# A tile's three partial products as three 256-column matmuls into one PSUM region, in place of 512 + 256 columns and a later add

## The chip, the core and the metric

The kernel runs on one NeuronCore of one Trainium2 chip. The metric is the device time of one execution in microseconds (us); three runs of the kernel before lie between 1150.1 and 1150.66 us, with a median of 1150.5 us. The profiler recorded one execution of its own, instruction by instruction.

## What is computed

One transformer-like layer on 256 rows of 2048 features, in float32 (B = 1, S = 256). Nearly all the arithmetic is in four weight matrices: `w_in` (2048 x 6676), `w_out` (2048 x 2048), `w_up` (2048 x 8192), `w_down` (8192 x 2048).

```python
h = rmsnorm(x, norm_mix)
proj = h @ w_in + b_in
...
x = x + jnp.concatenate([y_m, y_a, y_c], axis=-1) @ w_out
h2 = rmsnorm(x, norm_ffn)
x = x + jnp.square(jax.nn.relu(h2 @ w_up)) @ w_down
return rmsnorm(x, final_norm)
```

`y_m`, `y_a` and `y_c` are a chunked mLSTM of 8 heads, a forgetting attention of 4 heads and a convolution branch, all made from slices of `proj`.

## The kernel before

**Split operands.** A product has to come out to nearly float32 accuracy, while TensorE is fed the type fp32r. So every operand is split in a high part `hi` and a low part `lo` (the rest), and a product a·w is made of three partial products: a_hi·w_hi, a_lo·w_hi and a_hi·w_lo. The weights come from DRAM in pieces of 1 MiB (`unit`), by DMAs from the queue of SyncE. ScalarE copies half a piece to `hi` (line 368), VectorE subtracts to get `lo` (line 387). The activations are kept in a tile `big[name]` of 16 chunks (128 features each) by 512 columns: 256 rows' high parts, then the same 256 rows' low parts.

**Two kinds of block.** `Block` is a run of output columns that is accumulated in PSUM over the whole contraction; `matmuls` (lines 397 to 422) emits half a piece of it. In a block of kind A the activations are stationary and 512 columns of weights move; three matmuls of 512 columns go into one PSUM bank, two of them with the same stationary operand. In a block of kind B the weights are stationary (128 x 128 at a time, index `f`) and the activations move; the result is transposed, features by rows. Kind B serves the convolution branch, the queries and keys, the mLSTM's operands (all from `w_in`, blocks 256 wide, operand `x`) and the whole of `w_up` (blocks 512 wide, operand `h`). For each `f` and each chunk `k` a block of kind B issues two matmuls:

```python
mul(ps, hi[:, ii, f * P:(f + 1) * P], stat[:, k, :], s0, False)
mul(ps[:, 0:S], lo[:, ii, f * P:(f + 1) * P], stat[:, k, 0:S], False, s1)
```

The first streams all 512 columns (high and low rows) past w_hi, the second 256 columns past w_lo. Columns 0 to 255 of the bank then hold two of the partial products, columns 256 to 511 the third. So each `f` takes a bank of its own, and `join` (lines 434 to 453) adds the halves: ScalarE copies columns 256 to 511 to a tile `tmp` with bias and scale (line 441 or 443), VectorE adds columns 0 to 255 (line 447). For `w_up` four such joins make the tile `z`, VectorE makes relu(z)·z (line 1131), and the result is split again into the tile `hid`.

**Order of the work.** The kernel's own list scheduler (`task`, `best`, `issue`, `force`) gives each task to an engine at a time that it estimates from costs written in the code. The stream of weight pieces sets TensorE's order; small TensorE tasks (transposes, attention scores) are put between half pieces when their operands are expected to be there. PSUM has eight banks, in two rotations of four, `mm` and `mx`. Up to five split half pieces are held (`NHL`), and four raw pieces (`NRAW`).

Of the kernel before, what the change touches and what calls it, by code (L numbers as in the profile page):

```python
# [9 lines left out]
AF = mybir.ActivationFunctionType  # L10
# [23 lines left out]
def trunk(ctx: ExitStack, tc, x, norm_mix, w_in, b_in, mlstm_conv_w, mlstm_conv_b,  # L34
# [23 lines left out]

    # ---- emission: a list schedule on estimated engine clocks
    clock = dict(act=0.0, dve=0.0, pool=0.0, pe=0.0, ctl=0.0)  # L60
# [5 lines left out]
    class Buf:  # L66
        """One tile of a rotation of n: taken when the tile n before it has no readers left."""
        def __init__(self, rot):
# [39 lines left out]
    def room(takes):  # L108
        """When the buffers are free; None while a reader of the old tile is not yet issued."""
        r = 0.0  # L110
        for b in takes:
            h = b.rot.hist
            if len(h) >= b.rot.n:
                for u in h[len(h) - b.rot.n].readers:
                    if u.fin is None:
                        return None
                    r = max(r, u.fin + LAT)
        return r
# [54 lines left out]
    def extras():  # L173
        """TensorE tasks whose operands are there by now."""
        while True:
            run(clock["pe"])
            p = best("pe")
            if not p or p[2] > clock["pe"] - MARGIN:
                return
            issue(p[1], p[2])  # L180
# [12 lines left out]

    # ---- pools
    pools = {}
# [19 lines left out]

    # ---- loads of x, parameter rows
    RAWN = 8 * 272
# [31 lines left out]

    # x lies where the values and the attention operands come later  # L250
    xt = [sbt(pl("mix"), [P, 2 * NH * (HD + 1)], "x0", tag="vaug")[:, 0:D], sbt(pl("mix"), [P, D], "x1", tag="fqk")]
# [4 lines left out]

    # ---- constants
    ident = sbt(base, [P, P], "ident")
# [29 lines left out]
    def small(n=2):  # L288
        """Columns of the tile of statistics."""
        nst[0] += n  # L290
        return st[:, nst[0] - n:nst[0]]
# [3 lines left out]

    # ---- weight stream
    units = []

    class Block:
        def __init__(self, kind, w, st, key, tag="mm"):  # L300
            self.kind, self.w, self.st, self.key, self.tag = kind, w, st, key, tag
            self.n = 2 if kind == "A" else w // P
            self.bufs = [Buf(mm_rot if tag == "mm" else mx_rot) for _ in range(self.n)]
            self.done = [Task("pe", 0.0, None) for _ in range(self.n)]
            self.started = False
            self.need = {}

    def unit(b, src, c0, k0, last, gates=0, gside=None):
        """One MiB of weights: columns c0.. of src (and the gate columns beside them)."""
        n = 4 if b.w == 512 else 8  # L310
        units.append(dict(b=b, src=src, c0=c0, ks=list(range(k0, k0 + n)), w=b.w,
                          g=gates, gside=gside, last=last, first=not b.started))
        b.started = True
# [43 lines left out]
    def split_tasks(i, deps):  # L357
        """High and low parts of half a unit."""
        u, h = divmod(i, 2)
# [37 lines left out]
    def matmuls(i, toks):  # L397
        u, half = divmod(i, 2)
        d = units[u]
        b = d["b"]  # L400
        w = d["w"]
        n = len(d["ks"])
        stat = b.st()
        hi, lo = hl[i]
        for ii in range(n // 2):
            kk = half * (n // 2) + ii
            k = d["ks"][kk] % KC
            s0 = d["first"] and kk == 0
            s1 = d["last"] and kk == n - 1
            if b.kind == "A":  # L410
                for j in toks:
                    xh = stat[:, k, j * P:(j + 1) * P]
                    xl = stat[:, k, S + j * P:S + (j + 1) * P]
                    ps = b.bufs[j].t
                    mul(ps, xh, hi[:, ii, :], s0, False)
                    mul(ps, xh, lo[:, ii, :], False, False)
                    mul(ps, xl, hi[:, ii, :], False, s1)
            else:
                for f in range(w // P):
                    ps = b.bufs[f].t  # L420
                    mul(ps, hi[:, ii, f * P:(f + 1) * P], stat[:, k, :], s0, False)
                    mul(ps[:, 0:S], lo[:, ii, f * P:(f + 1) * P], stat[:, k, 0:S], False, s1)

# [6 lines left out]
    big_tile("y")  # L430
    chunk = {}   # tasks that make chunk k of a stationary or moving operand

    # rows of the transposed products, halves summed: out = s * (ps_a + ps_b) + bias
    def join(o, b, i, bias=None, s=1.0, prio=0, deps=(), takes=()):
        t = Buf(tmp_rot)
        pb = b.bufs[i]

        def f1():
            t.t = sbt(base, [P, S], "tmp", bufs=3)
            if bias is None:  # L440
                act.activation(t.t, pb.t[:, S:2 * S], AF.Copy)
            else:
                act.activation(t.t, pb.t[:, S:2 * S], AF.Identity, bias=bias, scale=s)  # L443

        def f2():
            if s == 1.0:
                dve.tensor_add(o(), t.t, pb.t[:, 0:S])
            else:
                dve.scalar_tensor_tensor(o(), pb.t[:, 0:S], s, t.t, op0=OP.mult, op1=OP.add)

        a = t_act(ca(S, True), f1, [b.done[i], col_tasks if bias is not None else None], prio=prio - 2,
                  takes=[t], uses=[pb])
        return t_dve(cd(S), f2, [a] + list(deps), prio=prio - 2, takes=takes, uses=[pb, t])

    # ---- parameter columns
    def cols_task(name, r0, r1, deps, prio=-3):
# [9 lines left out]

    # the array's clock rises once it is kept busy: transposes of the identity while x arrives
    def warm_up():
# [7 lines left out]

    # ---- x: norm, transpose, split
    xs_stat = [small(4) for _ in range(2)]
# [59 lines left out]

    # ---- late constants and parameters
    vb = {}  # L540
# [55 lines left out]

    # ---- values
    def blk(*a, **kw):
# [25 lines left out]

    # ---- conformer branch
    u_rot, g_rot = Rot(1), Rot(1)
# [99 lines left out]

    # ---- the other values, forgetting attention's operands
    b = block_units(blk("A", 512, xs, "x"), w_in, C_V + 512)
# [15 lines left out]

    # ---- gates
    gps, gsum, gtp = mx_buf(), mx_buf(), mx_buf()
# [13 lines left out]
    def build_gates():  # L760
# [11 lines left out]
        a_l = t_act(c1, lambda: act.activation(gl, gu, AF.Ln), [d_u], prio=3, table="ln")  # L772
        # log1p(e) = ln(u) + (e - (u - 1)) / u with u = fl(1 + e)
        d = t_dve(0.45, lambda: dve.scalar_tensor_tensor(ge, gu, -1.0, ge, op0=OP.add, op1=OP.subtract), [d_u], prio=3)
# [38 lines left out]

    # ---- heads, both kinds
    pw_rot, pt_rot, hh_rot = Rot(2), Rot(2), Rot(2)

    def head_out(num, nb, r, r_task, num_task, prio, put):
        """Root mean square norm of r * num by rows, transposed; put() takes the columns."""
        sq, t, sc = small(), small(), small()
# [30 lines left out]

    # ---- forgetting attention
    def fox(h, prio):
# [4 lines left out]
        def scores():  # L857
            q, k = hold["fqk"][:, h // 2, h % 2, :], hold["fqk"][:, 2 + h // 2, h % 2, :]
            ps = sb.t = bank("mx")
            # F[l] is constant along a row and leaves its softmax as it is: -F[s] and the mask are added  # L860
            mul(ps[:, 0:384], sel[:, NH + h:NH + h + 1].to_broadcast([P, P]), em, True, False)
            mul(ps[:, P:384], identb, mask_f.rearrange("p a b -> p (a b)"), False, False)
            mul(ps[:, 0:S], q[:, P:S], k, False, False)
            mul(ps[:, S:384], q[:, 0:P], k[:, 0:P], False, True)
# [39 lines left out]

    # ---- mLSTM
    xpad = [None, None]
# [124 lines left out]

    # ---- after the mixer
    ob = [blk("A", 512, ys, "y") for _ in range(4)]
# [66 lines left out]

    # ---- feed-forward layer, by quarters of the hidden features
    z_rot, zz_rot = Rot(2), Rot(2)
# [11 lines left out]
    for q in range(4):  # L1114
        down_of = []
        for c in range(4):
            b = block_units(blk("B", 512, lambda: big["h"], "h", tag()), w_up, 2048 * q + 512 * c)
            zb, wb = Buf(z_rot), Buf(zz_rot)

            def o_z(i, zb=zb):  # L1120
                if i == 0:
                    zb.t = sbt(pl("late"), [P, 4, S], "z", bufs=2)
                return zb.t[:, i, :]

            js = [late_open]
            for i in range(4):
                js.append(join(lambda i=i, o_z=o_z: o_z(i), b, i, takes=[zb] if i == 0 else [], deps=[js[-1]]))

            def f1(zb=zb, wb=wb):
                wb.t = sbt(pl("late"), [P, 4, S], "zz", bufs=2)  # L1130
                dve.scalar_tensor_tensor(wb.t, zb.t, 0.0, zb.t, op0=OP.max, op1=OP.mult)

# [62 lines left out]

    # ---- issue
    NU = len(units)
# [79 lines left out]
```

## Time and profile before

| | |
|---|---|
| Median of three runs | 1150.5 us |
| Span of the profiled execution, first to last instruction | 1148.2 us |
| TensorE (PE) busy | 1133.9 us, 99% |
| Weight loads (PEld) busy | 965.3 us, 84% |
| VectorE (DVE) busy | 717.3 us, 62% |
| ScalarE (ACT) busy | 574.3 us, 50% |
| Mean granted TensorE clock | 0.996 of full speed |
| Share of PE in the chain that ended last | 97% |

The profile gives the profiled execution by its span; the median of the runs is 2.3 us longer, which is taken here as what lies around the span. Every matmul shows as two records: a load of the stationary operand (LDWEIGHTS, under PEld) and the matmul (MATMUL, under PE). Records of matmuls overlap, since they are pipelined, so the length of a record is not what it costs: the cost in a stream is the distance from one start to the next.

### The profile page before, as it was taken

What the parts mean: (1) busy time and instruction counts of PE and PEld (TensorE: products, weight loads), DVE (VectorE), ACT (ScalarE), POOL (GpSimd) and SP (SyncE); (2) the same over time, 40 slices, a digit from 0 to 9 for tenths busy, and PEclk for the clock granted to TensorE, in tenths of its full rate; (3) what the DMA queues carried; (4) which work ended last, traced back from release to release, by engine and by line L of the source; (5) the groups of instructions that cost most, each with busy time, mean ns of one, the idle gap of its engine ahead of it and who ended that gap; (6) DMA issues with size and microseconds to landing.
All of it is one profiled execution on the core that took longest, in us unless ns stands there. A gap on an engine that the chain in (4) does not pass through costs nothing.

```text
span 1148.2 us, 14812 instructions
## 1 busy us (share of the span) xinstructions
PE 1133.9 (99%) x5880; PEld 965.3 (84%) x5880; DVE 717.3 (62%) x978; ACT 574.3 (50%) x807; POOL 17.6 (2%) x40
## 2 busy tenths in 40 slices
PE   8999999999999999999999999999999999999996
PEld 7888888888888888888888888888888888888885
DVE  6679988886665556556545655544655554566553
ACT  6455366777864545444344444333544333454442
POOL 1000000000000000000000000000000000000000
PEclk9999999999999999999999999999999999999999
DMA  8756654557546556655566655566655566655542
GB/s 304 242 184 191 199 164 148 151 153 248 169 162 220 184 185 184 190 199 196 184 189 193 189 193 190 184 191 195 189 193 187 184 192 199 190 189 184 183 147 74
DMA packets 127692, 214.91 MB, mean 187 GB/s; under 512 B 3676, under 2 KB 44936, under 8 KB 127240
## 3 DMA queue, kind: packets, MB, share of 16 engines
q1 hardware_dynamic: 127016, 212.92, 57.9%
q8 instruction: 46, 0.75, 0.3%
q10 hardware_dynamic: 608, 1.06, 0.3%
q14 instruction: 22, 0.18, 0.0%
HBM read 211.87 MB, written 2.10 MB: 186 GB/s over the span
## 4 chain that ended last, share of the span: by engine, by line
PE 97%; DMA 1%; issue 0%; ACT 0%; DVE 0%; SPq 0%; POOL 0%; POOLq 0%; ACTq 0%; DVEq 0%
PE mm L57 64%; PE mx L57 32%; DMA x<-in_x_dram 1%; PE mx L1085 0%; SPq L255 0%; PE mx L846 0%; POOL st L294 0%; PE mx L531 0%; ACT x2t L1188 0%; PE mx L879 0%; DVE lo L387 0%; ACT junk L1175 0%; POOLq L1272 0%; ACT hi L368 0%; PE mx L705 0%
## 5 line engine op out<-in xcount | busy, mean ns | idle before, releaser
L387 DVE TENSOR_TENSOR lo<-raw,hi 128x1024 fp32r<-128x1024 f32 x392 | 480.1, 1225 | 384.8 <-ACT hi L368 383.4
L368 ACT ACTIVATE hi<-raw 128x1024 fp32r<-128x1024 f32 x392 | 415.5, 1061 | 507.4 <-PE mm L57 317.8
L57 PE MATMUL mm<-x,hi 128*128 128x512 f32 x640 | 227.8, 400 | 0.0
L57 PE MATMUL mm<-h,hi 128*128 128x512 f32 x512 | 180.7, 397 | 0.0
L57 PE MATMUL mx<-h,hi 128*128 128x512 f32 x512 | 180.4, 397 | 0.0
L57 PE MATMUL mm<-x,lo 128*128 128x256 f32 x640 | 179.4, 280 | 0.0
L57 PE MATMUL mm<-hi,hid 128*128 128x512 f32 x512 | 159.0, 389 | 0.0
L57 PE MATMUL mx<-hi,hid 128*128 128x512 f32 x512 | 158.9, 389 | 0.0
L57 PEld LDWEIGHTS mm<-x,hi 128*128 128x128 f32 x640 | 120.2, 188 | 28.9 <-ACT tmp L443 0.4
L57 PE MATMUL mm<-h,lo 128*128 128x256 f32 x512 | 143.7, 281 | 0.0
L57 PE MATMUL mx<-h,lo 128*128 128x256 f32 x512 | 143.7, 281 | 0.0
L57 PEld LDWEIGHTS mm<-x,lo 128*128 128x128 f32 x640 | 120.9, 189 | 0.1
L57 PEld LDWEIGHTS mm<-h,hi 128*128 128x128 f32 x512 | 96.1, 188 | 23.3 <-DVE x2t L1073 0.2
L57 PEld LDWEIGHTS mx<-h,hi 128*128 128x128 f32 x512 | 96.1, 188 | 23.3
L57 PEld LDWEIGHTS mm<-hi,hid 128*128 128x128 f32 x512 | 96.1, 188 | 20.1
L57 PEld LDWEIGHTS mx<-hi,hid 128*128 128x128 f32 x512 | 96.1, 188 | 20.0
L57 PE MATMUL mm<-lo,hid 128*128 128x512 f32 x256 | 99.6, 389 | 0.0
L57 PE MATMUL mx<-lo,hid 128*128 128x512 f32 x256 | 99.6, 389 | 0.0
L57 PEld LDWEIGHTS mm<-h,lo 128*128 128x128 f32 x512 | 96.7, 189 | 0.2
L57 PEld LDWEIGHTS mx<-h,lo 128*128 128x128 f32 x512 | 96.7, 189 | 0.0
L57 PE MATMUL mm<-hi,y 128*128 128x512 f32 x256 | 80.4, 392 | 0.0
L57 PE MATMUL mm<-hi,x 128*128 128x512 f32 x192 | 61.6, 396 | 0.0
(191 smaller groups left out, 872.6 us busy)
## 6 DMA issues: line engine op xcount, KB each, us to landing
raw<-in_w_up_dram SPq DMA_DIRECT2D x64, 1024.0 KB, 5.3
raw<-in_w_down_dram SPq DMA_DIRECT2D x64, 1024.0 KB, 5.2
raw<-in_w_in_dram SPq DMA_DIRECT2D x45, 1024.0 KB, 5.3
raw<-in_w_out_dram SPq DMA_DIRECT2D x16, 1024.0 KB, 5.3
raw<-in_w_in_dram SPq DMA_DIRECT2D x4, 1032.0 KB, 5.1
raw<-in_w_in_dram SPq DMA_DIRECT2D x2, 1088.0 KB
x<-in_x_dram SPq DMA_DIRECT2D x8, 256.0 KB, 6.0
x2t<-in_x_dram SPq DMA_DIRECT2D x2, 1024.0 KB
```

Of the source, the lines that this page charges most:

```text
L57: pe.matmul(o, l, r, start=start, stop=stop, skip_group_check=True)
L368: act.activation(t, raws[u][0][:, h * n:(h + 1) * n, :], AF.Copy)
L387: dve.tensor_sub(hl[i][1], raws[u][0][:, h * n:(h + 1) * n, :], hl[i][0].bitcast(F32))
```

## The change

Blocks of kind B issue three matmuls of 256 columns per `f` and `k`, all into the same 256 columns of PSUM: w_hi past the high rows, w_hi past the low rows, w_lo past the high rows. Two `f` share a bank, so a block takes half as many banks. `join` becomes one ScalarE activation with bias and scale, straight from PSUM to its target. For `w_up` ScalarE applies Relu to two `f` at once (512 columns), and VectorE squares with a plain product.

```diff
         def __init__(self, kind, w, st, key, tag="mm"):
             self.n = 2 if kind == "A" else w // P
-            self.bufs = [Buf(mm_rot if tag == "mm" else mx_rot) for _ in range(self.n)]
+            banks = 2 if kind == "A" else self.n // 2
+            self.bufs = [Buf(mm_rot if tag == "mm" else mx_rot) for _ in range(banks)]
...
                 for f in range(w // P):
-                    ps = b.bufs[f].t
-                    mul(ps, hi[:, ii, f * P:(f + 1) * P], stat[:, k, :], s0, False)
-                    mul(ps[:, 0:S], lo[:, ii, f * P:(f + 1) * P], stat[:, k, 0:S], False, s1)
+                    ps = b.bufs[f // 2].t[:, (f % 2) * S:(f % 2 + 1) * S]
+                    wh, wl = (t[:, ii, f * P:(f + 1) * P] for t in (hi, lo))
+                    mul(ps, wh, stat[:, k, 0:S], s0 and f % 2 == 0, False)
+                    mul(ps, wh, stat[:, k, S:2 * S], False, False)
+                    mul(ps, wl, stat[:, k, 0:S], False, s1)
...
-    def join(o, b, i, bias=None, s=1.0, prio=0, deps=(), takes=()):
-        t = Buf(tmp_rot)
-        pb = b.bufs[i]
+    def join(o, b, i, bias, s=1.0, prio=0, deps=(), takes=()):
+        pb = b.bufs[i // 2]
         def f1():
-            t.t = sbt(base, [P, S], "tmp", bufs=3)
-            if bias is None:
-                act.activation(t.t, pb.t[:, S:2 * S], AF.Copy)
-            else:
-                act.activation(t.t, pb.t[:, S:2 * S], AF.Identity, bias=bias, scale=s)
-
-        def f2():
-            if s == 1.0:
-                dve.tensor_add(o(), t.t, pb.t[:, 0:S])
-            else:
-                dve.scalar_tensor_tensor(o(), pb.t[:, 0:S], s, t.t, op0=OP.mult, op1=OP.add)
+            act.activation(o(), pb.t[:, (i % 2) * S:(i % 2 + 1) * S], AF.Identity, bias=bias, scale=s)
...
-            for i in range(4):
-                js.append(join(lambda i=i, o_z=o_z: o_z(i), b, i, takes=[zb] if i == 0 else [], deps=[js[-1]]))
+            for i in range(2):
+                def f0(i=i, zb=zb, pb=b.bufs[i]):
+                    if i == 0:
+                        zb.t = sbt(pl("late"), [P, 4, S], "z", bufs=2)
+                    act.activation(zb.t[:, 2 * i:2 * i + 2, :], pb.t.rearrange("p (c s) -> p c s", c=2), AF.Relu)
...
-                dve.scalar_tensor_tensor(wb.t, zb.t, 0.0, zb.t, op0=OP.max, op1=OP.mult)
+                dve.tensor_mul(wb.t, zb.t, zb.t)
```

TensorE, at the start of the first `w_up` block (`mm` is a PSUM bank, `h` the activations, `hi` and `lo` the weights' parts, then partitions x columns of the output); before:

```order
L57 MATMUL mm<-hi,y 128x512
L57 MATMUL mm<-h,hi 128x512
L57 MATMUL mm<-h,lo 128x256
L57 MATMUL mm<-h,hi 128x512
L57 MATMUL mm<-h,lo 128x256
```

and with the change:

```order
L57 MATMUL mm<-hi,y 128x512
L57 MATMUL mm<-h,hi 128x256 x2
L57 MATMUL mm<-h,lo 128x256
L57 MATMUL mm<-h,hi 128x256 x2
L57 MATMUL mm<-h,lo 128x256
```

Each matmul of 512 columns has become two of 256; the built program has 7475 matmul instructions where it had 5811, that is 1664 more. Around the blocks the small tasks of the mixer stand a few half pieces earlier or later, and their number is the same.

VectorE, at the end of the first `w_up` block (`z` holds a block's sums, `zz` the squares, `hid` the split result); before:

```order
L387 TENSOR_TENSOR lo<-raw,hi 128x1024 x6
L447 TENSOR_TENSOR z<-tmp,mm 128x256 x4
L1131 SCALAR_TENSOR_TENSOR zz<-z 128x1024
L387 TENSOR_TENSOR lo<-raw,hi 128x1024 x2
L1137 TENSOR_TENSOR hid<-zz,hid 128x4x256
```

and with the change (line 388 is the former 387, 1124 the former 1131, 1130 the former 1137):

```order
L388 TENSOR_TENSOR lo<-raw,hi 128x1024 x6
L1124 TENSOR_TENSOR zz<-z 128x1024
L388 TENSOR_TENSOR lo<-raw,hi 128x1024 x2
L1130 TENSOR_TENSOR hid<-zz,hid 128x4x256
```

The four additions are gone and the square stays in its place.

ScalarE at the same place; before:

```order
L368 ACTIVATE hi<-raw 128x1024 x6
L441 ACTIVATE tmp<-mm 128x256 x4
L368 ACTIVATE hi<-raw 128x1024 x2
L1135 ACTIVATE hid<-zz 128x4x256
```

and with the change:

```order
L369 ACTIVATE hi<-raw 128x1024 x6
L1117 ACTIVATE z<-mm 128x512 x2
L369 ACTIVATE hi<-raw 128x1024 x2
L1128 ACTIVATE hid<-zz 128x4x256
```

Four copies of 256 columns have become two activations of 512, between the same splits.

## Rows read from the trace of the kernel before

**Rows 1.** The page's first part: busy us (share of the span) and instructions.
```profile
PE 1133.9 (99%) x5880; PEld 965.3 (84%) x5880; DVE 717.3 (62%) x978; ACT 574.3 (50%) x807; POOL 17.6 (2%) x40
```

**Rows 2.** Waits of PE, then of PEld: us in total, times, longest.
```profile
PE mx L531 <- DVE x L511: 3.6, 1, 3.6
...
PEld mm L57 <- DVE lo L387: 0.6, 1, 0.6
```

**Rows 3.** The page's costliest groups: xcount | busy us, mean ns of a record.
```profile
L57 PE MATMUL mm<-x,hi 128*128 128x512 f32 x640 | 227.8, 400 | 0.0
...
L57 PE MATMUL mx<-h,hi 128*128 128x512 f32 x512 | 180.4, 397 | 0.0
...
L57 PE MATMUL mm<-hi,hid 128*128 128x512 f32 x512 | 159.0, 389 | 0.0
...
L57 PEld LDWEIGHTS mm<-hi,hid 128*128 128x128 f32 x512 | 96.1, 188 | 20.1
```

**Rows 4.** The chain that ended last: start us, us, what, xmatmuls.
```profile
207.99 16.96 PE mm L57 x96
...
272.98 8.32 PE mm L57 x48
...
346.24 1.34 PE mx L57 x12
...
452.89 22.19 PE mx L57 x128
...
541.25 21.76 PE mx L57 x96
...
629.13 22.61 PE mx L57 x128
```

**Rows 5.** Timeline of PE from 500 us: start us, length us, what.
```profile
500.10 0.28 PE L57 MATMUL mx<-h,lo 128*128 128x256 f32 x1
500.22 0.39 PE L57 MATMUL mx<-h,hi 128*128 128x512 f32 x1
500.45 0.28 PE L57 MATMUL mx<-h,lo 128*128 128x256 f32 x1
500.57 0.39 PE L57 MATMUL mx<-h,hi 128*128 128x512 f32 x1
```

**Rows 6.** Timeline of PE from 650.4 us.
```profile
650.40 0.28 PE L57 MATMUL mx<-h,lo 128*128 128x256 f32 x1
650.52 0.40 PE L57 MATMUL mx<-h,hi 128*128 128x512 f32 x1
650.76 0.28 PE L57 MATMUL mx<-h,lo 128*128 128x256 f32 x1
650.88 0.40 PE L57 MATMUL mx<-h,hi 128*128 128x512 f32 x1
```

**Rows 7.** Timeline of the weight loads (PEld) from 500 us.
```profile
500.11 0.19 PEld L57 LDWEIGHTS mx<-h,hi 128*128 128x128 f32 x1
500.22 0.19 PEld L57 LDWEIGHTS mx<-h,lo 128*128 128x128 f32 x1
```

**Rows 8.** Groups by form, ScalarE and VectorE at the joins.
```profile
L1131 DVE SCALAR_TENSOR_TENSOR zz<-z 128x1024 f32<-128x1024 f32 x16 | 19.6, 1225 | 0.5
...
L443 ACT ACTIVATE tmp<-mm,colp 128x256 f32<-128x256 f32 x36 | 15.3, 472 | 17.7 <-PE mm L57 17.7
...
L447 DVE TENSOR_TENSOR z<-tmp,mm 128x256 f32<-128x256 f32 x32 | 11.8, 422 | 0.0
L441 ACT ACTIVATE tmp<-mx 128x256 f32<-128x256 f32 x32 | 11.5, 385 | 6.5 <-PE mx L57 6.5
...
L937 ACT ACTIVATE mqk<-mqk 128x512 f32<-128x512 f32 x8 | 5.0, 624 | 0.0
```

**Rows 9.** Timeline of PE from 346 us.
```profile
346.08 1.50 PE L57 MATMUL mx<-vaug,pt 128*128 128x129 f32 x12
347.33 0.48 PE L57 MATMUL mm<-hi,y 128*128 128x512 f32 x1
```

More of the change, by code (lines that the diff above doesn't have):

```diff
@@ L431, in trunk @@
     chunk = {}
-    def join(o, b, i, bias=None, s=1.0, prio=0, deps=(), takes=()):
-        t = Buf(tmp_rot)
-        pb = b.bufs[i]
+    def join(o, b, i, bias, s=1.0, prio=0, deps=(), takes=()):
+        pb = b.bufs[i // 2]
         def f1():
-            t.t = sbt(base, [P, S], "tmp", bufs=3)
-            if bias is None:
-                act.activation(t.t, pb.t[:, S:2 * S], AF.Copy)
-            else:
-                act.activation(t.t, pb.t[:, S:2 * S], AF.Identity, bias=bias, scale=s)
-        def f2():
-            if s == 1.0:
-                dve.tensor_add(o(), t.t, pb.t[:, 0:S])
-            else:
-                dve.scalar_tensor_tensor(o(), pb.t[:, 0:S], s, t.t, op0=OP.mult, op1=OP.add)
-        a = t_act(ca(S, True), f1, [b.done[i], col_tasks if bias is not None else None], prio=prio - 2,
-                  takes=[t], uses=[pb])
-        return t_dve(cd(S), f2, [a] + list(deps), prio=prio - 2, takes=takes, uses=[pb, t])
+            act.activation(o(), pb.t[:, (i % 2) * S:(i % 2 + 1) * S], AF.Identity, bias=bias, scale=s)
+        return t_act(ca(S, True) + 0.09, f1, [b.done[i], col_tasks] + list(deps), prio=prio - 2, takes=takes,
+                     uses=[pb])
     def cols_task(name, r0, r1, deps, prio=-3):
@@ L1118, in trunk @@
             zb, wb = Buf(z_rot), Buf(zz_rot)
[L1120 to L1123, printed above, removed]
             js = [late_open]
-            for i in range(4):
-                js.append(join(lambda i=i, o_z=o_z: o_z(i), b, i, takes=[zb] if i == 0 else [], deps=[js[-1]]))
+            for i in range(2):
[3 more added lines that the diff above has]
+                    act.activation(zb.t[:, 2 * i:2 * i + 2, :], pb.t.rearrange("p (c s) -> p c s", c=2), AF.Relu)
+                js.append(t_act(ca(512, True), f0, [b.done[2 * i], b.done[2 * i + 1], js[-1]], prio=-2,
+                                takes=[zb] if i == 0 else [], uses=[b.bufs[i]]))
             def f1(zb=zb, wb=wb):
                 wb.t = sbt(pl("late"), [P, 4, S], "zz", bufs=2)
-                dve.scalar_tensor_tensor(wb.t, zb.t, 0.0, zb.t, op0=OP.max, op1=OP.mult)
+                dve.tensor_mul(wb.t, zb.t, zb.t)
             d = t_dve(cd(1024), f1, js[1:], prio=-1.9, takes=[wb], uses=[zb])
```

## Prediction, made before the changed kernel ran

> **What bounds the kernel.** I read the page's busy shares first: PE is busy 99% of the span, VectorE 62%, ScalarE 50% [rows 1]. Records of matmuls overlap, so a busy PE alone proves little; the waits settle it. In the whole execution PE waited once for longer than 2 us, for the first scaled rows of x at the start, and no weight load of the main stream waited longer than 0.6 us for a split weight [rows 2]. So nothing feeds TensorE too late, and the end is set by how many matmuls it has to stream and how far apart they start. The chain that ended last gives that distance, since its pieces are unbroken runs of one kind [rows 4].
>
> Kind A, 512 columns each: 96 matmuls in 21.76 us, so 226.7 ns apart [rows 4]. Kind B runs in two rhythms. In the first quarter of `w_up` 64 pairs of 512 + 256 columns take 22.19 us, 346.7 ns a pair; in the later quarters 22.61 us, 353.3 ns a pair [rows 4]. The blocks of `w_in` show the same two (8.32 us for 24 pairs is 346.7 ns, 16.96 us for 48 pairs is 353.3 ns) [rows 4]. There are 640 + 512 + 512 = 1664 pairs, with as many of `mm<-h,hi` as of `mx<-h,hi` [rows 3]. Going through the chain I count 400 at 346.7 ns (256 in the first quarter, 144 in `w_in`) and 1264 at 353.3 ns: 585.3 us in all, a mean of 351.7 ns. Half of the kernel is the thing that is changed.
>
> **The change, part by part.**
>
> *Columns.* A tile has 768 columns to stream before and after. At the granted full clock of 2.4 GHz that is 320.0 ns, so the columns themselves neither gain nor lose.
>
> *Matmuls and loads.* Two become three: 1664 more matmuls, and 1664 more loads, because this program loads the stationary operand again even where it stays the same: in kind A, where two of three matmuls have the same one, there are 512 loads for 512 matmuls of `hi,hid` [rows 3]. What is the cost of one more start? 512 columns are 213.3 ns and take 226.7, so 13.3 ns come on top per matmul in kind A [rows 4]. If that is a cost per matmul, a pair should cost 320.0 + 2 x 13.3 = 346.7 ns, which is exactly the quicker rhythm [rows 4]. That two kinds of stream give the same figure is why I take it. A triple then costs 320.0 + 3 x 13.3 = 360.0 ns, 120.0 ns for each matmul of 256 columns. Against the mean of 351.7 that is 8.3 ns a tile; 1664 x 360.0 = 599.0 us, less 585.3, is **13.8 us** more. All of it is on the path, as there is no wait of TensorE in which it could hide [rows 2].
>
> The trace of before has no run of 256-column matmuls, so I bound it. From below: twelve fp32 matmuls of 129 columns, each with its own load, stream at 1.34 us / 12 = 111.7 ns [rows 4, 9], and three of these are 335 ns. From above: in the slower rhythm, if kind A's 226.7 ns is taken off for the long matmul, 126.7 ns are left for the short one, and three of these are 380 ns [rows 4]. Over all tiles these ends are -27.7 us and +47.1 us. Between them the short matmul's own slot, start to start, is 0.12 us in both rhythms [rows 5, 6], which 360 ns fits best of the round figures.
>
> The Trainium skill, "TensorE: Matmul & The Clock Gate", section "Back-to-back issue gap", has a smaller price: a warm matmul is followed by the next after N / 2.4 + 2.5 ns, so a third one would cost 2.5 ns, and the sum would be 1664 x 2.5 = 4.2 us by an estimate from that page. Kind A's rows say 13.3 ns where the page says 2.5, so the rows decide; both speak against the change.
>
> *Joins.* VectorE loses 104 additions (40 of `w_in`, 64 of `w_up`) at 422 ns, 43.9 us; ScalarE loses 64 copies at 385 ns, 24.6 us, and gets 32 activations of 512 columns, for which the nearest row is 624 ns, 20.0 us; its 40 joins with a bias go on at about 472 ns, and the square is one pass over 1024 elements as before, 1225 ns [rows 8]. All of this costs and gains **nothing**: VectorE and ScalarE have 38% and half of the span free and TensorE waits for neither [rows 1, 2]. The cover is the stream of matmuls, and it gets longer. If ScalarE's reading of a bank were late, the next block of the same rotation would wait; but a block now takes one or two of four banks where it took two or four, so there is more room, not less.
>
> *Small tasks.* The mixer's transposes and scores stand at other places between the half pieces, some groups in two. The long matmul behind such a group shows a record of 0.48 us, some 0.09 us over its fellows' 0.39 [rows 3, 9]; three more of these would be 0.3 us, which I leave out of the sum. Start and tail hold no block of kind B.
>
> *Sum.* 1150.5 + 13.8 = **1164.3 us**. The terms come from the profiled execution, whose span is 1148.2 us, 2.3 below the median of the runs; I add the difference to the median. For the forecast itself I allow 356 to 364 ns a triple: 1158 to 1171 us.
>
> **The rivals.**
>
> *Faster: the overhead is per column.* 226.7 / 213.3 is also 17/16, and 17/16 of 256 columns is 113.3 ns. Then three short matmuls cost 340.0 ns and the pairs' other 7 to 13 ns come from the alternation of long and short, which goes away when all are alike; kind A is uniform and keeps one rhythm, while the pairs keep two [rows 4]. 1664 x 340.0 is 565.8 us, so 1131.0 us. For it: the uneven slots in the slower rhythm (0.24 us for the long matmul, where kind A needs 0.227) [rows 4, 6]. Against it: the quicker rhythm is even too, and it is 6.7 ns over this rule [rows 4, 5]. It decides where a short matmul starts less than 351.7 / 3 = 117.2 ns behind the last. Chance 17%.
>
> *No change: the short slot as it stands.* A short matmul's slot is rounded to 0.12 us; in the quicker rhythm a pair is 0.347 by the chain, of which the timeline gives 0.23 to the long one, so the short one may be 0.117 [rows 4, 5]. Three of these are 351 ns, 584.1 us, 1149.3 us. Chance 15%.
>
> *Much slower: the load is the bound.* A load starts with the matmul ahead of it [rows 5, 7], so it has only that matmul's time. Behind a long matmul it has 227 ns, behind a short one 113 to 120. Before, every second load is short of time; after, every one. If that is what makes 346.7 into 353.3, each short slot becomes 126.7 ns: 380 ns a triple, 632.3 us, 1197.6 us. For it: the load's record is 188 ns, longer than the slot [rows 3, 7]. Against it: such records overlap without harm at 111.7 ns in the fp32 stream [rows 4, 9]. The same page of the Trainium skill, section "LDWEIGHTS (loading the stationary operand)", puts a load of 128 columns at 107 ns, which would fit; no row here shows a load's bare time. Chance 13%.
>
> *The change does not do what it says: the second load is left out.* If the same w_hi were kept and the overhead belonged to the load, a triple would cost 320.0 + 2 x 13.3 = 346.7 ns, 1142.2 us. Kind A's count of loads speaks against it [rows 3]. Chance 5%.
>
> **How the numbers follow.** The forecast has the other 50%. The range runs from the first rival's 1131 to 1178 us, which is 368 ns a triple, two fifths of the way from the forecast to the load-bound end; it leaves out that end's 13% and some 5% at the lower one. Differences within 0.2% (2.3 us) are about what a measurement here cannot tell from no change. Faster: 17 + 5 + 3 of the no-change rival's 15 = 25%. Same: 10 of that 15. Slower: 50 + 13 + its last 2 = 65%.
>
> **What would show it.** In the changed kernel's chain a block of `w_up` is 192 matmuls; the forecast has them in 23.0 us, the first rival in 21.8, the no-change rival in 22.5, the load-bound one in 24.3. Kind A should stay at 21.76 us for 96. As many loads as matmuls should stand on the page, some 7540 (5880 + 1664). VectorE should be busy some 44 us less with TensorE still unwaiting; a new wait of TensorE for a bank or for a split would make the sum wrong from another side. The step that everything hangs on is that the 13.3 ns belong to a matmul, not to its columns.

## The result, and the profile after

The changed kernel takes 1164.9 us (four runs, 1164.67 to 1165.46) against 1150.58 us beside it: a ratio of 1.0124, 95% interval 1.011 to 1.0138. It is 1.2% slower; 1164.3 us was forecast. The span of the profiled execution is 1162.7 us, 14.5 more than before.

The page of the changed kernel, busy time by engine, to be read against [rows 1]:

```profile
PE 1146.7 (99%) x7544; PEld 1054.6 (91%) x7544; DVE 680.3 (59%) x874; ACT 569.4 (49%) x775; POOL 19.5 (2%) x40
```

There are 1664 more matmuls and 1664 more loads. VectorE has 104 instructions and 37.0 us less, and none of that came back as time. The chain that ended last in the changed kernel (start us, us, what, xmatmuls), to be read against [rows 4]:

```profile
248.34 17.26 PE mm L57 x144
...
459.62 23.04 PE mx L57 x192
...
550.53 21.76 PE mx L57 x96
...
638.85 23.04 PE mx L57 x192
```

A block of `w_up` is now 23.04 us for 192 matmuls, exactly 120.0 ns from start to start, and the same in the first quarter and in a later one (459.62 and 638.85). In `w_in` 144 matmuls take 17.26 us, 119.9 ns each. The two rhythms of before have become one. Kind A is as it was: 21.76 us for 96. The timeline of the changed kernel's PE shows the even steps:

```profile
500.02 0.28 PE L57 MATMUL mm<-h,lo 128*128 128x256 f32 x1
500.14 0.40 PE L57 MATMUL mm<-h,hi 128*128 128x256 f32 x2
500.38 0.28 PE L57 MATMUL mm<-h,lo 128*128 128x256 f32 x1
```

The two `hi` matmuls of a tile stand in one row; from 500.02 to 500.38 is one tile, 0.36 us. PE's waits in the changed kernel, to be read against [rows 2]:

```profile
PE mx L523 <- DVE x L503: 5.3, 1, 5.3
PE mm L463 <- POOL gb L272: 1.4, 1, 1.4
```

The second of these stands in the kernel before as well:

```profile
PE mm L471 <- POOL gb L272: 1.4, 1, 1.4
```

No wait has come up in the stream. The one at the start is 1.7 us longer than before; it lies ahead of every changed matmul and waits for the first rows of x. It is between 3.1 and 5.6 us in the traces of this case, the unchanged kernel at 3.6 and one with old joins and old banks at 4.4, so it is not put down to the change here. The mean granted clock is 0.995 where it was 0.996, so the clock does not explain the loss. With the tiles' 13.8 us it makes 15.5 us, where the span grew by 14.5; the remaining -1.0 us lies in the small work around and was not followed further.

### The profile page after: what moved, and what is told of

Read it like the earlier page. It is cut to its first block, busy times and chain, and to the rows that moved or that the text cites. A ratio compares the mean times of both kernels' runs of the same rounds, so it can differ in the third digit from the quotient of the medians.

```text
span 1162.7 us, 18014 instructions
## 1 busy us (share of the span) xinstructions
PE 1146.7 (99%) x7544; PEld 1054.6 (91%) x7544; DVE 680.3 (59%) x874; ACT 569.4 (49%) x775; POOL 19.5 (2%) x40
## 4 chain that ended last, share of the span: by engine, by line
PE 98%; DMA 1%; issue 0%; SPq 0%; ACT 0%; DVE 0%; POOLq 0%; POOL 0%; ACTq 0%; DVEq 0%
PE mm L57 64%; PE mx L57 32%; DMA x<-in_x_dram 1%; PE mx L523 0%; PE mx L1077 0%; SPq L255 0%; PE mx L838 0%; ACT x2t L1181 0%; PE mx L871 0%; ACT junk L1168 0%; POOLq L1265 0%; POOL st L294 0%; PE mx L697 0%; PE mx L669 0%; DVE djunk L481 0%
## 5 line engine op out<-in xcount | busy, mean ns | idle before, releaser
L57 PE MATMUL mm<-x,hi 128*128 128x256 f32 x1280 | 233.1, 284 | 0.0
L57 PEld LDWEIGHTS mm<-x,hi 128*128 128x128 f32 x1280 | 199.3, 191 | 0.7 <-issue 0.4
L57 PE MATMUL mm<-h,hi 128*128 128x256 f32 x1024 | 184.7, 283 | 0.0
L57 PE MATMUL mx<-h,hi 128*128 128x256 f32 x1024 | 184.7, 283 | 0.0
L57 PEld LDWEIGHTS mm<-h,hi 128*128 128x128 f32 x1024 | 160.0, 192 | 0.3
L57 PEld LDWEIGHTS mx<-h,hi 128*128 128x128 f32 x1024 | 159.7, 192 | 0.0
```

Of the source, the lines that this page charges most:

```text
L57: pe.matmul(o, l, r, start=start, stop=stop, skip_group_check=True)
```

## The experiments

The question was what the 8.3 ns a tile are: a start's fixed cost (the theory), the columns, the load, the shared region of PSUM, or the joins.

### The matmuls alone

The three matmuls of 256 columns, in the old banks and with the old joins:

```diff
-                    mul(ps, hi[:, ii, f * P:(f + 1) * P], stat[:, k, :], s0, False)
-                    mul(ps[:, 0:S], lo[:, ii, f * P:(f + 1) * P], stat[:, k, 0:S], False, s1)
+                    wh, wl = (t[:, ii, f * P:(f + 1) * P] for t in (hi, lo))
+                    mul(ps[:, 0:S], wh, stat[:, k, 0:S], s0, False)
+                    mul(ps[:, S:2 * S], wh, stat[:, k, S:2 * S], False, False)
+                    mul(ps[:, 0:S], wl, stat[:, k, 0:S], False, s1)
```

> The matmul part alone: three matmuls of 256 columns, but each tile keeps its own bank with two halves, and the old joins (ScalarE copy, VectorE add) stay. Theory of starts (each start costs a fixed 13.3 ns and nothing else of the change matters): 120.0 ns a matmul, a w_up block of 192 in 23.04 us, about 1164.5 us. Rival, the shared PSUM region (accumulating three times in a row into the same 256 columns is what costs): here the middle matmul goes to other columns, so a part of the 8.3 ns a tile goes away, and the time falls towards 1151 us. Rival, joins: if part of the loss came from the new joins, it would fall below 1164 as well.

Measured: 1164.99 us, ratio to before 1.0126 (1.011 to 1.0143). A block in this kernel's chain:

```profile
459.93 23.04 PE mx L57 x192
```

The whole loss is there without the shared region and without the new joins. Both rivals fall.

### The joins alone

```diff
-                    ps = b.bufs[f // 2].t[:, (f % 2) * S:(f % 2 + 1) * S]
+                    ps = b.bufs[f // 2].t
...
-                    mul(ps, wh, stat[:, k, 0:S], s0 and f % 2 == 0, False)
-                    mul(ps, wh, stat[:, k, S:2 * S], False, False)
-                    mul(ps, wl, stat[:, k, 0:S], False, s1)
+                    mul(ps, wh, stat[:, k, :], s0 and f % 2 == 0, False)
+                    mul(ps[:, (f % 2) * S:(f % 2 + 1) * S], wl, stat[:, k, 0:S], False, s1)
```

> The join part alone: new joins and shared banks, with the old two matmuls (512 + 256 columns) a tile; the 512-column matmul writes over both tiles of a bank, so the sums are mixed. Theory of starts: TensorE's stream is as before, 351.7 ns a tile on average, so 1150.5 us within 0.2%; VectorE some 40 us less busy. Rival, joins help or hurt: another time than 1150.5 by more than 0.2%.

Measured: 1150.22 us, ratio 0.9999 (0.999 to 1.0008). The page's busy line of this kernel:

```profile
PE 1133.2 (99%) x5880; PEld 965.4 (84%) x5880; DVE 680.2 (59%) x874; ACT 570.1 (50%) x775; POOL 19.5 (2%) x40
```

VectorE's 37 us are saved here too, and no change of time is seen.

### Two matmuls of equal length

```diff
-                    mul(ps, hi[:, ii, f * P:(f + 1) * P], stat[:, k, :], s0, False)
-                    mul(ps[:, 0:S], lo[:, ii, f * P:(f + 1) * P], stat[:, k, 0:S], False, s1)
+                    mul(ps[:, 0:384], hi[:, ii, f * P:(f + 1) * P], stat[:, k, 0:384], s0, False)
+                    mul(ps[:, P:2 * S], lo[:, ii, f * P:(f + 1) * P], stat[:, k, P:2 * S], False, s1)
```

> Before, with the 768 columns of a tile cut into 384 + 384 in place of 512 + 256 (some products are then left out and others done twice). Theory of starts: (160.0 + 13.3) x 2 = 346.7 ns a tile, in one even rhythm, a w_up block of 128 in 22.19 us, 1142 us. Rival, overhead per column (17/16) with a floor of 120 ns for a slot with a load: 170.0 x 2 = 340.0 ns, a block in 21.76 us, 1131 us. If the slower rhythm (353.3 ns) has nothing to do with the short matmul, it stays here too, and the time is near 1150 us.

Measured: 1143.73 us, ratio 0.9941 (0.9921 to 0.9961). A block in this kernel's chain:

```profile
473.70 22.19 PE mm L57 x128
```

22.19 us for 128 is 173.4 ns a matmul: 160.0 for the columns and 13.4 on top. The theory's figure holds at 256, 384 and 512 columns; 17/16 per column (170.0) does not. And the slower rhythm is gone, in all quarters, though starts and columns are as many as before: it goes with the unequal pair.

### Four matmuls of 192 columns

```diff
-                    mul(ps, wh, stat[:, k, 0:S], s0 and f % 2 == 0, False)
-                    mul(ps, wh, stat[:, k, S:2 * S], False, False)
-                    mul(ps, wl, stat[:, k, 0:S], False, s1)
+                    mul(ps[:, 0:192], wh, stat[:, k, 0:192], s0 and f % 2 == 0, False)
+                    mul(ps[:, 64:S], wh, stat[:, k, 64:S], False, False)
+                    mul(ps[:, 0:192], wl, stat[:, k, 0:192], False, False)
+                    mul(ps[:, 64:S], wl, stat[:, k, 64:S], False, s1)
```

> After, with four matmuls of 192 columns a tile (768 columns as before, overlapping halves, so sums are mixed). Theory of starts: 4 x (80.0 + 13.3) = 373.3 ns a tile, 1187 us. Rival, the load is the floor: a slot can't be shorter than some 112 to 120 ns, since the next load needs that long: 4 x 112 to 4 x 120 = 448 to 480 ns a tile, 1311 to 1364 us. A slot between them gives the load's bare time.

Measured: 1308.62 us in a single run. A block in this kernel's chain:

```profile
520.75 28.59 PE mx L57 x256
```

111.7 ns a slot (from one start to the next) where the theory has 93.3. At 192 columns something else sets the slot; it is the figure that the fp32 stream of before showed [rows 4, 9]. Where it takes over was not measured; 13.3 ns on top of the columns would come down to 111.7 at some 236 columns, by estimate.

### A load of half the width

Here only 64 of the 128 weight columns are loaded, in all chunks of a block but the first, first with the changed kernel's three matmuls, then with the pair of before:

```diff
+                    h = slice(0, P) if s0 else slice(0, 64)
-                    ps = b.bufs[f // 2].t[:, (f % 2) * S:(f % 2 + 1) * S]
-                    wh, wl = (t[:, ii, f * P:(f + 1) * P] for t in (hi, lo))
+                    ps = b.bufs[f // 2].t[h, (f % 2) * S:(f % 2 + 1) * S]
+                    wh, wl = (t[:, ii, f * P:f * P + h.stop] for t in (hi, lo))
```

> After, with 64 of a tile's 128 weight columns loaded for all chunks but the first. Theory of starts: the slot of a matmul of 256 columns stays at 120.0 ns, as its 13.3 ns belong to a start and not to the load's length: a w_up block near 23.04 us, 1164.5 us. Rival, the load sets the slot: the slot falls to some 109 to 113 ns, a block to 21.0 to 21.8 us, and the time to 1114 to 1133 us.

> Before, with only 64 of a tile's 128 weight columns loaded for all chunks but the first (the sums of the other features are left short). Columns streamed and starts are as before. If the slower rhythm comes from the load behind the short matmul, a load of half the width has time to spare, and all pairs take 346.7 ns: 1142 us. If the rhythm has nothing to do with the load's length, both rhythms stay: about 1150 us.

Measured: 1134.69 us for the three, 1131.49 us for the pair, a single run each. Chain of the kernel with three matmuls and half loads:

```profile
469.32 21.84 PE mm L57 x192
```

and of the one with the pair and half loads:

```profile
619.34 21.79 PE mx L57 x128
...
532.25 21.76 PE mx L57 x96
```

The theory falls in its plain form: with the starts unchanged the mean slot of 256 columns drops from 120.0 to 113.8 ns. That mean still holds the block's first chunk, one in sixteen, with full loads. Its 12 matmuls at 120.0 ns taken off, the other 180 are at 113.3 ns. A start's overhead is not fixed: 6.7 of the 13.3 ns at 256 columns go with the load's width. But it isn't the load alone either. The pair's block less four full tiles at 346.7 ns leaves 340.1 ns for a tile, of which a short slot of 113.3 leaves 226.8 for the long one, within 0.1 of kind A's figure with a full load: by this subtraction the half load saves nothing at 512 columns. The timeline agrees to its hundredths, 0.23 us behind a long matmul and 0.11 behind a short one:

```profile
629.74 0.39 PE L57 MATMUL mx<-h,hi 128*64 128x512 f32 x1
629.97 0.27 PE L57 MATMUL mx<-h,lo 128*64 128x256 f32 x1
630.08 0.39 PE L57 MATMUL mx<-h,hi 128*64 128x512 f32 x1
```

No stream of long matmuls alone was run with half loads. The slower rhythm goes away as well, now without a change of lengths (619.34 lies in a later quarter). One rival is left in these runs: half a load also writes only 64 of the bank's 128 partitions, and none of them tells the two apart.

### A load of three quarters

The slots so far fit one rule, made from them: N columns take N cycles of 2.4 GHz and on top the greater of N / 16 and a quarter of the loaded columns. Its test is the same edit with `slice(0, 96)`:

> After, with 96 of a tile's 128 weight columns loaded for all chunks but the first. The slots so far follow one rule: N columns take N cycles of 2.4 GHz and, on top, the greater of N / 16 and a quarter of the loaded columns. By that rule a slot of 256 columns with a load of 96 is 256 + 24 cycles, 116.7 ns: a w_up block of 192 in 22.4 us, about 1150 us. If there is a threshold in place of a slope: 120.0 ns (23.04 us) or 113.3 ns (21.8 us).

Measured: 1145.6 us in a single run, and in this kernel's chain:

```profile
473.77 22.31 PE mm L57 x192
```

116.2 ns a slot, or 115.9 without the first chunk's full loads, against the rule's 116.7: between 113.3 and 120.0, so a slope and not a threshold. The time is 4 us under the expectation because the rule's 22.4 us was turned into a total too loosely; 1664 x 3 x 116.2 = 580.1 us is 5.2 less than the 585.3 of before, which gives 1145.4.

### 192 columns with half a load

> Four matmuls of 192 columns a tile as in the run four_192, with 64 of a tile's 128 weight columns loaded for all chunks but the first. If the 111.7 ns floor of that run is the time of a load of 128 columns, half a load has a lower floor, and by the rule (192 + 16 cycles) a slot is 86.7 ns: a w_up block of 256 in 22.2 us, about 1142 us. If the floor belongs to a load and a matmul as such, whatever their width, the slot stays at 111.7 ns: a block in 28.6 us, 1309 us.

Measured: 1164.23 us in a single run. A block in this kernel's chain:

```profile
482.29 23.07 PE mm L57 x256
```

The mean slot falls from 111.7 to 90.1 ns, or 88.7 without the first chunk (16 of the 256 matmuls, at 111.7), so the floor goes with the width of the load and does not belong to a load and a matmul as such. It does not fall to the rule's 86.7; the rule is good to 0.8 ns at 256 columns and misses by 2.0 here.

### Other orders of the pair

Two long matmuls of neighbouring tiles, then their two short ones:

```diff
-                for f in range(w // P):
-                    ps = b.bufs[f].t
-                    mul(ps, hi[:, ii, f * P:(f + 1) * P], stat[:, k, :], s0, False)
-                    mul(ps[:, 0:S], lo[:, ii, f * P:(f + 1) * P], stat[:, k, 0:S], False, s1)
+                for f0 in range(0, w // P, 2):
+                    for f in (f0, f0 + 1):
+                        mul(b.bufs[f].t, hi[:, ii, f * P:(f + 1) * P], stat[:, k, :], s0, False)
+                    for f in (f0, f0 + 1):
+                        mul(b.bufs[f].t[:, 0:S], lo[:, ii, f * P:(f + 1) * P], stat[:, k, 0:S], False, s1)
```

> Before, with the same matmuls in another order: the two long ones (512 columns) of two neighbouring tiles, then their two short ones (256 columns). Starts and columns are the same in number, so by the theory of starts alone a tile costs 346.7 ns, if nothing disturbs it: 1142 us. If the slower rhythm (353.3 ns) comes from the alternation of long and short at each start, it goes away here: 1142 us. If it comes from each load behind a short matmul being short of time, there are as many of these as before (one per tile) and the time stays at 1150.5 us.

Measured: 1144.84 us, ratio 0.9949 (0.9932 to 0.9966). This is the fastest of the kernels that do all of the work, faster than the kernel before and the changed one. Its chain, first and later quarter:

```profile
473.40 22.30 PE mm L57 x128
...
649.63 22.29 PE mm L57 x128
```

348.3 ns a tile, in every quarter. As many loads stand behind a short matmul as before, so the plain count of such loads, the second explanation on record, does not decide. The first, that each change of length costs, was tried with longer runs: all long ones of a chunk and then the short ones, and the same over half a piece.

> Before, with all long matmuls of a chunk first (four tiles in w_up, two in w_in), then their short ones. A long slot is 226.7 ns and a short one 120.0 in an even run. If a change of length between neighbours is what costs, there are fewer of them: w_up falls from 348.3 ns a tile (two and two) to 347 to 347.5 ns, a block of 128 in 22.2 us, w_in stays as with two and two; about 1143 to 1144.5 us. If the order is indifferent beyond the alternation of one and one: 1144.8 us as with two and two. If four short ones in a row add up their lateness: back towards 1150 us.

> Before, with the eight long matmuls of a half piece first, then the eight short ones, in w_up and in w_in. If a change of length between neighbours is what costs: 346.7 to 347 ns a tile everywhere, a w_up block of 128 in 22.2 us, 1142 to 1143 us. If the order is indifferent: 1144.8 us.

Measured: 1148.94 us, ratio 0.9982 (0.9973 to 0.9991), and 1148.13 us, ratio 0.9973 (0.9963 to 0.9984). The chain with all long ones of a chunk first:

```profile
650.88 22.45 PE mm L57 x128
```

and with those of half a piece first:

```profile
652.59 22.35 PE mm L57 x128
```

350.8 and 349.2 ns a tile of `w_up`: fewer changes of length, and slower than two and two. That explanation falls too. All orders are better than one and one in its slower rhythm, none reaches 346.7; what locks the stream into a rhythm stays open.

### The low part in bf16

```diff
-            hl[i] = [t, sbt(base, [P, n, d["w"]], "lo", F32R, bufs=NHL)]
+            hl[i] = [t, sbt(base, [P, n, d["w"]], "lo", BF, bufs=NHL)]
...
-                    mul(ps[:, 0:S], lo[:, ii, f * P:(f + 1) * P], stat[:, k, 0:S], False, s1)
+                    mul(ps[:, 0:S], lo[:, ii, f * P:(f + 1) * P], st16[:, k, :], False, s1)
```

> Before, with the low part of the weights kept in bf16 and streamed against a bf16 copy of the activations, one more ScalarE pass for the copy and four split half pieces held in place of five; the other two partial products stay fp32r, and the third is rounded to bf16. If the 13.3 ns belong to any start, whatever the type: kind A stays at 226.7 ns a matmul and a pair at 347 to 353 ns, 1142 to 1152 us. If they belong to fp32r: the bf16 matmuls cost less, kind A's 512 columns down to 213.3 to 217 ns for a third of them (up to 10 us over 736), the short ones of 1664 tiles down to the load floor of 112 ns (up to 14 us against 120): 1120 to 1140 us. If ScalarE's extra copies make TensorE wait, it shows as waits for hi or lo.

Measured: 1170.56 us, ratio 1.0172 (1.0157 to 1.0187): slower, which neither side had. Chain, a block of kind B and one of kind A (two records are missing in the latter):

```profile
483.21 22.93 PE mm L57 x128
...
529.08 22.18 PE mm L57 x94
```

The weight loads of this kernel, in order of time, with the gap before one of them in brackets:

```profile
500.48 0.10 PEld L57 LDWEIGHTS <-lo 128*128 128x128 bf16 x1
500.48 0.20 PEld L57 LDWEIGHTS mm<-h,hi 128*128 128x128 f32 x1
500.84 0.10 PEld L57 LDWEIGHTS <-lo 128*128 128x128 bf16 x1 [0.15 <-issue]
```

and the long matmul ahead of the first of them:

```profile
500.17 0.47 PE L57 MATMUL mm<-h,hi 128*128 128x512 f32 x1
```

The bf16 load does not start with the long matmul ahead of it, as the fp32r load does [rows 5, 7]; it starts at 500.48, 0.31 us behind that matmul's start and together with the next load. Why is not shown. TensorE waits for `lo` once, for 0.4 us, so ScalarE's extra copies are not the cause. A tile costs 358.3 ns, and a kind A block takes 22.18 us in place of 21.76. So this run does not tell what a bf16 start would cost in a stream of its own type.

## Why the prediction was right

**What bounds the kernel** was right: in all the kernels tried the time follows the distance between TensorE's starts. No trace has a wait of TensorE over 1.4 us besides that for the first rows of x, and the mean granted clock is 0.995 to 0.997 in all.

**The price of a tile** was right to 0.1 ns: 360.0 forecast, 23.04 us / 64 = 360.0 measured; the mean of before, 351.7, came from the chain, and the difference of the two over 1664 tiles carries 13.8 of the 14.3 us between the medians.

**The reason given for the price** was only half right. The step "the 13.3 ns belong to a matmul, not to its columns" holds at 256, 384 and 512 columns with a load of 128, and that is all that the change needed. With a load of 64 a start at 256 columns costs 6.7 ns, and at 512 still 13.3 by subtraction. The rule that fits these slots is a share of the columns or a share of the load, whichever is greater; with a load of 128 its second share is 32 cycles, 13.3 ns, at every width up to 512, which is why kind A and the quicker pair agreed on one figure. So the agreement was not proof of a cost per matmul. It was also one of sums alone: within the quicker pair the starts are 0.23 us and some 0.117 apart, not 226.7 and 120.0 ns, as the no-change rival pointed out. That 120.0 would hold in a uniform stream was a bet, and it was given 50%. The first rival (per column) has 113.3 ns, which came out with half the load; the load-bound rival was right that there is a floor, 111.7 ns at 192 columns. Neither gave the time.

**The load as the bound** was mis-sized: a slot with a full load can be as short as 111.7 ns (192 columns), so three slots of 120 have room for it and do not grow to 126.7. That 126.7 was a remainder and no slot of the rows: in the slower rhythm the short slot stays at 0.12 us and the long one grows from 0.23 to 0.24 [rows 5, 6]. In these runs the slower rhythm needs an unequal pair, one and one, and a full load together.

**The small price of a start** from the Trainium skill, "TensorE: Matmul & The Clock Gate", section "Back-to-back issue gap" (N / 2.4 + 2.5 ns), is not what this stream shows at any length: 13.3 ns at 256, 384 and 512 columns. The section gives that formula for an isolated matmul and says that in a stream of loads and matmuls both set the spacing, which the prediction left out and which the slots of 120.0, 115.9 and 113.3 ns with loads of 128, 96 and 64 columns agree with. Its section "LDWEIGHTS (loading the stationary operand)" has P / 1.2 ns for P columns, 107 ns for 128 by an estimate from that page. That is near the 111.7 ns floor, and the floor's fall with half a load agrees that the width counts.

**The joins** were rightly priced at nothing (0.9999). VectorE's 44 us less came out as 37.0: the estimate multiplied the mean length of a record, and records overlap, as the row itself shows (32 records of 422 ns would be 13.5 us and are busy for 11.8) [rows 8].

**The second load left out** was not what happened: 7544 loads for 7544 matmuls. No kernel here left a load out, so what a start costs without one is not known.

## What to carry to other kernels

Price a matmul stream by the distance between starts in an unbroken run, not by the columns nor by the record lengths, and look for a second kind of stream that gives the same overhead per start. Where a stream of matmuls is the bound, do not cut a matmul in two to save work on engines that nobody waits for. Two prices that agree at one size may still have two causes: vary the load's width and the length apart before the figure is used elsewhere.

## What the runs showed that was not expected

- The overhead of a start goes with the load's width at 256 columns: with loads of 128, 96 and 64 weight columns a slot takes 120.0, 115.9 and 113.3 ns. At 512 columns it does not seem to: 226.7 ns with a load of 128, and 226.8 by subtraction with one of 64.
- A stream of 192 columns with full loads runs at 111.7 ns a slot, with half loads at 88.7.
- The same long and short matmuls in another order are worth 0.5% of the kernel: in `w_up` two and two take 348.3 ns a tile, eight and eight 349.2, four and four 350.8, one and one 346.7 or 353.3 by rhythm.
- In the one stream with a bf16 matmul between fp32r ones, its load starts only with the load after it, and a pair costs 358.3 ns.
